# A layer of hybrid RG-LRU and neighbourhood attention on one core: 36 weight loads go from SyncE's queue to ScalarE's

## The chip, the core and the metric

The kernel runs on one core of a Trainium2 chip. The metric is the time of one execution in device microseconds (us), the median over several runs. Engines are called by the names that the profile uses: PE (TensorE, matrix products; PEld are its weight loads), DVE (VectorE), ACT (ScalarE), POOL (GpSimd) and SP (SyncE, which here only issues DMA transfers). SPq is SP's queue of instructions.

## The reference

One layer over 512 tokens of 1024 features, in float32:

```python
x = x + 0.5 * swiglu_1(rmsnorm(x))
h = rmsnorm(x)
xr, gr, q, k, v, ga, gb = split(h @ w_in, 7)      # 1024 columns each
xc = conv4(xr)                                    # centred, depthwise
y_lru = (scan_forward(xc) + scan_backward(xc)) * gelu(gr)
q = rmsnorm_per_head(q) * 64**-0.5; k = rmsnorm_per_head(k)
y_att = neighbourhood_attention(q, k, v, rel_pos_bias)  # 16 heads, window 8 rows x 16 columns
x = x + (sigmoid(ga) * y_lru + sigmoid(gb) * y_att) @ w_out
x = x + 0.5 * swiglu_2(rmsnorm(x))
```

## The kernel before

Features lie on the 128 partitions and tokens along the row. Every float32 operand of a product is split into a rounded high part and a low rest, and each product is three matrix products (high by high, high by low, low by high). The weights come in chunks of 128 x 1024 (512 KB). `load_w` (lines 159 to 169) loads one: a DMA fills a raw buffer, ACT casts it to the high part `wh` (line 145) and DVE subtracts to get the low part `wl` (line 148). There are three raw buffers and four pairs of `wh` and `wl`. So the load of chunk i waits until the `wl` of chunk i-3 is made, and the cast of chunk i waits until TensorE is done with chunk i-4; if nothing holds the loads back, up to seven chunks are on their way or ready ahead of TensorE.

The layer runs in stages: the first feed-forward block, the projection xr with its convolution, then q, k and v in two halves of eight heads (`hf` 0 and 1, lines 1101 to 1111; 12 chunks in each half), then the three gates (`gates`, line 1114: 24 chunks `wg`, 8 each for gr, ga and gb), w_out, and the second feed-forward block. The scans and the attention are laid between the chunks: `weave` (line 577) takes so many steps of each of five lists after each chunk and in its middle, at rates set by hand for each stage.

The attention of one half (`heads`, line 937) makes four tiles of two heads each (`fi` 0 to 3). For a tile, ACT and DVE split q and k into `qh`, `ql`, `kh`, `kl` (lines 961 to 966), TensorE makes the scores (line 989), DVE and ACT the softmax (lines 1009 to 1021), DVE transposes the result (lines 1030, 1031), SP writes it to memory (`pd<-pt`, line 1033), POOL reads it back turned (`PT<-pd`, line 1037), TensorE applies it to v (line 1052), and ACT copies the result out (`att`, line 1062). In the second half q and k are not turned on TensorE: DVE transposes blocks (line 916), SP writes them to memory (`qd`, line 919), and SP fetches each tile two tiles ahead (`xqk<-qd`, line 933, four DMAs for each tile).

The order of instructions on each engine's queue is settled when the program is built: a planner walks the program and at each moment gives an engine the ready instruction that stands first in the program, except those put under a high priority, by its own reckoning of times. The casts and subtractions of `load_w` have high priority; its DMA has not. On the chip every queue keeps that order, and an instruction that has to wait holds all that stand behind it in its queue. In the kernel before, SP's queue holds nearly all loads of weights (line 163), the writes of v (line 863), `qd` (919), the fetches of q and k (933) and the writes of the softmax (1033).

Of the kernel before, what the change touches and what calls it, by code (L numbers as in the profile page):

```python
# [91 lines left out]
def block_kernel(ctx: ExitStack, tc, a, out):  # L92
    nc = tc.nc
# [14 lines left out]
    def nm(s):  # L108
        uid[0] += 1
        return f"{s}_{uid[0]}"  # L110
# [32 lines left out]
    def split(raw, H, L, act=True):  # L143
        if act:
            nc.scalar.activation(H, raw, AF.Copy)  # L145
        else:
            nc.vector.tensor_copy(H, raw)
        return nc.vector.tensor_tensor(L, raw, H.bitcast(F32), ALU.subtract)  # L148

    nld = [0]  # L150

    def raw_t():
        return wpool.tile([P, 1024], F32, tag="wraw", bufs=3, name=nm("wraw"))

    def hl_t():
        return (wpool.tile([P, 1024], F32R, tag="wh", bufs=4, name=nm("wh")),
                wpool.tile([P, 1024], F32R, tag="wl", bufs=4, name=nm("wl")))

    def load_w(src, n, act=True):
        raw = raw_t()  # L160
        H, L = hl_t()
        s = slice(0, n)
        ld = nc.sync.dma_start(raw[:, s], src[:, s])
        if nld[0] < 8:
            tc.keep_in_program_order(ld)
        nld[0] += 1
        with tc.high_priority():
            split(raw[:, s], H[:, s], L[:, s], act)
        return H, L
# [6 lines left out]
    def feat_chunk(src, nk, xh, xl, ps, k0, ktot, act=True, mid=None):  # L176
        H, L = load_w(src, nk * P, act)
        for k in range(nk):
            s = slice(k * P, (k + 1) * P)
            kk = k0 + k  # L180
            mm3(ps, H[:, s], L[:, s], xh[kk], xl[kk], kk == 0, kk == ktot - 1)
            if mid is not None and k == nk // 2 - 1:
                weave(mid)
# [241 lines left out]
    def ffn(wgu, ws, wd, xh, xl, S, ssum, plain, res, emit_out, lead=None, end=None):  # L425
# [86 lines left out]
        for q in range(2):  # L512
# [19 lines left out]
            for j in range(FT // 2):  # L532
                ws_.append(load_w(wd[q, j], 1024))
                ahead(q * FT + 2 * j + 2 + AHEAD)
                if j < FT // 2 - DTAIL:
                    for k in (2 * j, 2 * j + 1):
                        for i in range(4):
                            put_in(i, k)
# [58 lines left out]
    def load_pairs():  # L597
        for k in range(KT):
            if k % 2 == 0:
                q = pair_t()  # L600
            xres[k] = q[:, k % 2]
# [107 lines left out]
    def lru():  # L709
# [14 lines left out]
        def fetch(f):  # L724
            wts[f] = load_w(a["wgate"][f], 2 * P)
# [115 lines left out]
    def qk_raw(w, hf, st):  # L841
        raws = []
        for ps in tok_group(w, hf):
            t = big_t(n="qk")
            with tc.high_priority():
                copy = nc.scalar.activation(t, ps, AF.Copy)  # L846
            raws.append(t)
        for j, t in enumerate(raws):
            sq = big.tile([P, T], F32, tag="pt", bufs=2, name=nm("sq"))
            after(nc.scalar.activation(sq, t, AF.Square), copy)  # L850
            nc.vector.reduce_sum(st[:, w, j, :], sq.rearrange("p (h d) -> p h d", d=HD), axis=AX.X)
        weave(RATE[phase[0]])
        return raws

    def v_get(hf):
        for j, ps in enumerate(tok_group(2, hf)):
            t = big_t(n="v")
            with tc.high_priority():
                nc.vector.tensor_scalar(t, ps, rcol[:, j : j + 1], None, ALU.mult)
            V[hf, 2 * j] = t  # L860

        for j in range(NCB):
            nc.sync.dma_start(vd[hf][:, j * QC : (j + 1) * QC, :], V[hf, 2 * j])
        lanes["v"].append(v_more(hf))
        if hf == 0:
            until("v", lambda: False)
        weave(RATE[phase[0]])
# [31 lines left out]
    def norm_qk(raws, st, qd):  # L899

        rq = tiny.tile([P, 2, NCB, 8], F32, tag="rq", name=nm("rq"))
        for w in range(2):
            for j in range(NCB):
                hold(nc.vector.tensor_scalar(rq[:, w, j, :], st[:, w, j, :], 1.0 / HD, epsv[:, j : j + 1],
                                             ALU.mult, ALU.add))
        hold(nc.scalar.activation(rq, rq, AF.Sqrt))
        nc.vector.reciprocal(rq, rq)
        yield
        for j in range(NCB):
            for w in range(2):  # L910
                t = raws[w][j].rearrange("p (h d) -> p h d", d=HD)
                hold(nc.vector.tensor_tensor(t, t, rq[:, w, j, :].unsqueeze(2).to_broadcast([P, 8, HD]), ALU.mult))
            if qd is not None:
                t2 = pair_t().rearrange("p a b -> p (a b)")
                for w in range(2):
                    nc.vector.transpose(
                        t2.rearrange("p (c f w i) -> p w f c i", c=NCB, f=4, w=2)[:, w],
                        raws[w][j].rearrange("p (f c i) -> p f c i", c=NCB, i=32))
                nc.sync.dma_start(qd[j], t2)
                yield  # L920
            elif j % 2 == 1:
                yield
        if qd is not None:
            yield
            fetch(qd, 0)
            fetch(qd, 1)
# [174 lines left out]
    for hf in range(2):  # L1101
        st = tiny.tile([P, 2, NCB, 8], F32, tag="st", name=nm("st"))
        raws = [qk_raw(0, hf, st), qk_raw(1, hf, st)]
        if hf == 1:
            qd = dram.tile([NCB, P, NCB, 4, 64], F32, name="qd")
            lanes["prep"].append(norm_qk(raws, st, qd))
        v_get(hf)
        if hf == 0:
            lanes["att"].append(norm_qk(raws, st, None))
        lanes["att"].append(heads(hf, raws, qd if hf == 1 else None))  # L1110
        phase[0] = "t1" if hf == 0 else "g"


    def gates(w, fs, fn, scale=1.0):
# [34 lines left out]
            yl.append(L)  # L1149


    nxt = {}
    load_pairs()
    forms = Forms(C_G2)
# [103 lines left out]
```

## Time and profile before

| | us |
|---|---|
| median of 3 runs | 1118.76 |
| lowest and highest run | 1116.25, 1119.7 |
| the profiled execution, its own time | 1117.62 |
| its span, first to last instruction | 1115.8 |
| PE busy | 1096.9 (98%) |
| ACT busy | 619.1 (55%) |

The profile is of one execution. In the views below, a start is in us from the start of the span. A timeline merges instructions of one kind that follow each other, with their count. Issuing a DMA is not counted as busy time of an engine. What stands in brackets is the time for which the engine was idle before the instruction, and what ended it. The granted clock is the share of TensorE's full clock: 1.00 is 2.4 GHz, 0.50 is 1.2 GHz.

### The profile page before, as it was taken

How to read it: one execution, taken by the hardware profiler on the slowest of the kernel's cores; microseconds unless marked ns; L12 is line 12 of the kernel's file. 1: busy time of each engine (PE TensorE's matmuls, PEld its weight loads, DVE VectorE, ACT ScalarE, POOL GpSimd, SP SyncE). 2: the span in 40 equal slices, each digit the busy share in tenths (PEclk: the TensorE clock that was granted, in tenths of full speed). 3: DMA queues.
4: the chain of work that ended last, by engine and by line, in shares of the span. 5: the costliest groups of instructions: out<-in, count | busy, mean ns of one | idle time of the engine just before them, and what ended most of it. 6: DMA issues, size and time to landing. Idle time of an engine off the chain costs nothing.

```text
span 1115.8 us, 17664 instructions
## 1 busy us (share of the span) xinstructions
PE 1096.9 (98%) x6779; PEld 971.5 (87%) x6779; DVE 796.1 (71%) x1228; ACT 619.1 (55%) x950; POOL 140.0 (13%) x243
## 2 busy tenths in 40 slices
PE   9999999999999999999999699999999999999998
PEld 8899999988888778787878488888999999998887
DVE  7777777794745877998786474759877777784642
ACT  8554554563533768877688482446645444564330
POOL 0000000000000441241226320001000000000000
PEclk9999999999999999999999799999999999999999
DMA  8566666643423685674789853376756666653421
GB/s 268 151 169 152 154 152 167 167 136 95 135 87 112 173 234 157 179 197 128 231 266 231 251 183 128 105 246 156 197 147 162 155 167 147 157 169 95 132 76 38
DMA packets 68451, 180.02 MB, mean 161 GB/s; under 512 B 17680, under 2 KB 21264, under 8 KB 68368
## 3 DMA queue, kind: packets, MB, share of 16 engines
q1 hardware_dynamic: 52160, 131.94, 36.4%
q0 software_dynamic: 15632, 46.70, 20.9%
q8 instruction: 53, 0.87, 0.3%
q10 hardware_dynamic: 576, 0.26, 0.1%
q14 instruction: 30, 0.25, 0.1%
HBM read 152.63 MB, written 17.83 MB: 153 GB/s over the span
## 4 chain that ended last, share of the span: by engine, by line
PE 93%; DVE 3%; ACT 2%; DMA 2%; issue 1%; SPq 0%; DVEq 0%; ACTq 0%
PE acc L312 31%; PE acc L172 10%; PE acc L174 9%; PE acc L173 9%; PE aux L312 5%; PE acc L834 4%; PE aux L173 4%; PE aux L172 4%; PE aux L174 4%; PE acc L835 4%; PE acc L836 4%; PE aux L742 1%; PE aux L1052 1%; DMA vd<-v 1%; ACT p L1021 1%
## 5 line engine op out<-in xcount | busy, mean ns | idle before, releaser
L145 ACT ACTIVATE wh<-wraw 128x1024 fp32r<-128x1024 f32 (+3 forms) x236 | 233.3, 991 | 322.2 <-issue 88.7
L148 DVE TENSOR_TENSOR wl<-wraw,wh 128x1024 fp32r<-128x1024 f32 (+3 forms) x236 | 267.5, 1137 | 111.4 <-ACT wh L145 107.7
L312 PE MATMUL acc<-s,wh 128*128 128x256 f32 x1280 | 232.2, 283 | 0.0
L312 PEld LDWEIGHTS acc<-s,wh 128*128 128x128 f32 x1280 | 199.7, 192 | 0.0
L312 PE MATMUL acc<-s,wl 128*128 128x256 f32 x640 | 181.1, 283 | 0.0
L312 PEld LDWEIGHTS acc<-s,wl 128*128 128x128 f32 x640 | 122.9, 192 | 0.0
L172 PE MATMUL acc<-xh,wh 128*128 128x512 f32 x272 | 108.6, 399 | 10.8 <-ACT wh L145 10.8
L174 PE MATMUL acc<-xh,wl 128*128 128x512 f32 x272 | 107.2, 394 | 0.0
L173 PE MATMUL acc<-xl,wh 128*128 128x512 f32 x272 | 107.0, 393 | 0.0
L312 PE MATMUL acc<-xh,wl 128*128 128x256 f32 x320 | 90.6, 283 | 0.0
L312 PE MATMUL acc<-xl,wh 128*128 128x256 f32 x320 | 90.6, 283 | 0.0
L312 PE MATMUL acc<-xh,wh 128*128 128x256 f32 x320 | 90.6, 283 | 0.0
L834 PE MATMUL acc<-wh,xh 128*128 128x512 f32 x192 | 75.7, 394 | 1.0 <-ACT qk L846 1.0
L148 DVE TENSOR_TENSOR hl<-h,hh 128x512 fp32r<-128x512 f32 x88 | 57.3, 686 | 25.4 <-PE aux L173 23.4
L835 PE MATMUL acc<-wh,xl 128*128 128x512 f32 x192 | 74.8, 390 | 0.0
L836 PE MATMUL acc<-wl,xh 128*128 128x512 f32 x192 | 74.7, 389 | 0.0
L172 PEld LDWEIGHTS acc<-xh,wh 128*128 128x128 f32 x272 | 51.7, 190 | 23.7 <-ACT wh L145 11.0
L172 PE MATMUL aux<-hh,wh 128*128 128x512 f32 (+1 forms) x181 | 69.9, 386 | 0.0
L173 PE MATMUL aux<-hl,wh 128*128 128x512 f32 (+1 forms) x181 | 69.9, 386 | 0.0
L174 PE MATMUL aux<-hh,wl 128*128 128x512 f32 (+1 forms) x181 | 69.9, 386 | 0.0
L174 PE MATMUL acc<-hh,wl 128*128 128x512 f32 (+1 forms) x176 | 67.9, 386 | 0.0
L173 PE MATMUL acc<-hl,wh 128*128 128x512 f32 (+1 forms) x176 | 67.9, 386 | 0.0
(226 smaller groups left out, 2301.8 us busy)
## 6 DMA issues: line engine op xcount, KB each, us to landing
wraw<-wqkv SPq DMA_DIRECT2D x24, 512.0 KB
wraw<-wg SPq DMA_DIRECT2D x24, 512.0 KB
wraw<-w1d SPq DMA_DIRECT2D x22, 512.0 KB
wraw<-w2s SPq DMA_DIRECT2D x22, 512.0 KB
pair<-w2s SPq DMA_DIRECT2D x22, 512.0 KB
wraw<-w2d SPq DMA_DIRECT2D x22, 512.0 KB
wraw<-w1s SPq DMA_DIRECT2D x18, 512.0 KB
pair<-w1s SPq DMA_DIRECT2D x18, 512.0 KB
```

The lines of the kernel that those rows point to most:

```text
L145: nc.scalar.activation(H, raw, AF.Copy)
L148: return nc.vector.tensor_tensor(L, raw, H.bitcast(F32), ALU.subtract)
L172: nc.tensor.matmul(ps, wh, xh, start=first, stop=False, skip_group_check=skip)
L173: nc.tensor.matmul(ps, wh, xl, start=False, stop=False, skip_group_check=skip)
L174: mark["mm"] = nc.tensor.matmul(ps, wl, xh, start=False, stop=last, skip_group_check=skip)
L312: mm = nc.tensor.matmul(o, w_[:, c], x_, start=first and m + k == 0 and w_ is H and x_ is xh_, stop=m + k == 4 and w_ is L, skip_group_che ...
L742: prev, mm = mm, nc.tensor.matmul(ps[d][b], W[w][o, c], X[x][o], start=x == 1, stop=w + x == 0)
L834: nc.tensor.matmul(pss[j], xh[kk][:, tj], H[:, s], start=kk == 0, stop=False)
L835: nc.tensor.matmul(pss[j], xl[kk][:, tj], H[:, s], start=False, stop=False)
L836: mark["mm"] = nc.tensor.matmul(pss[j], xh[kk][:, tj], L[:, s], start=False, stop=kk == KT - 1)
L1021: nc.scalar.activation(pt, pt, AF.Copy, scale=rs[:, hp, n : n + 1])
L1052: mm = nc.tensor.matmul(pv[h2 * HD : (h2 + 1) * HD, n * P : (n + 1) * P], vt[:, (fi * 2 + h2) * HD : (fi * 2 + h2 + 1) * HD], PT[:, q], st ...
```

## The change

The queue from which `load_w` issues its DMA becomes a variable: SP's as before, but from the end of the first half's pass (after its q, k, v and the start of its attention) ACT's, and SP's again ahead of w_out. So the 12 loads of the second half's q, k and v and the 24 loads of the gates are issued by ACT. The small loads of the scans' weights (`wgate`, line 725) go through `load_w` too; their last issue in the trace before lies at 431.7 us, ahead of the second half's first load. Buffers, dependences and the rest of the program are the same.

```diff
@@ -148,6 +148,7 @@
     nld = [0]
+    wq = [nc.sync]
@@ -160,7 +161,7 @@
         raw = raw_t()
         H, L = hl_t()
         s = slice(0, n)
-        ld = nc.sync.dma_start(raw[:, s], src[:, s])
+        ld = wq[0].dma_start(raw[:, s], src[:, s])
@@ -1109,6 +1110,7 @@
         lanes["att"].append(heads(hf, raws, qd if hf == 1 else None))
         phase[0] = "t1" if hf == 0 else "g"
+        wq[0] = nc.scalar
@@ -1149,6 +1151,7 @@
+    wq[0] = nc.sync
     nxt = {}
     load_pairs()
     forms = Forms(C_G2)
```

## Rows read from the trace of the kernel before

**Rows 1.** The page, parts 1 and 2: engine, busy us, share; then tenths in 40 slices.

```profile
PE 1096.9 (98%) x6779; PEld 971.5 (87%) x6779; DVE 796.1 (71%) x1228; ACT 619.1 (55%) x950; POOL 140.0 (13%) x243
...
PEclk9999999999999999999999799999999999999999
```

**Rows 2.** Waits of TensorE, 440 to 735 us: who waited for whom, us, times, longest.

```profile
PE acc L172 <- ACT wh L145: 10.8, 1, 10.8
PE aux L1052 <- issue: 1.9, 1, 1.9
PE acc L834 <- ACT qk L846: 1.0, 1, 1.0
PE aux L989 <- DVE kl L966: 0.3, 1, 0.3
```

**Rows 3.** Timeline of TensorE, 590 to 660 us: start us, us, instruction, [idle before it].

```profile
594.47 0.40 PE L989 MATMUL aux<-kl,qh 64*128 64x256 f32 x2 [0.32 <-DVE kl L966]
...
629.25 0.80 PE L172 MATMUL acc<-xh,wh 128*128 128x512 f32 x1 [10.78 <-ACT wh L145]
...
634.88 0.39 PE L172 MATMUL acc<-xh,wh 128*128 128x512 f32 x1
...
640.10 0.39 PE L174 MATMUL acc<-xh,wl 128*128 128x512 f32 x1
```

**Rows 4.** Stretches: busy us (instructions) of PE, PEld, DVE, ACT, POOL; granted clock; DMA share; GB/s.

```profile
575.00:585.00 10.00, 10.00 (x53) 8.01 (x52) 7.97 (x23) 9.57 (x19) 0.61 (x1) 1.00 1.00 319
585.00:595.00 10.00, 9.68 (x49) 7.77 (x49) 7.80 (x17) 8.57 (x18) 6.41 (x11) 1.00 0.80 225
595.00:605.00 10.00, 10.00 (x84) 8.50 (x82) 5.90 (x26) 9.92 (x27) 6.50 (x11) 1.00 1.05 237
...
622.00:630.00 8.00, 0.75 (x2) 0.50 (x2) 3.29 (x6) 1.06 (x1) 3.36 (x7) 0.50 1.01 346
```

**Rows 5.** Timeline of SyncE, 440 to 700 us: start us, us over all, DMA issues merged.

```profile
573.49 0.33 SPq L163 DMA_DIRECT2D wraw<-wg  x1
578.52 0.32 SPq L933 DMA_DIRECT2D xqk<-qd  x1
...
579.42 7.68 SPq L933 DMA_DIRECT2D xqk<-qd  x7
...
594.44 2.39 SPq L933 DMA_DIRECT2D xqk<-qd  x4
...
607.02 2.31 SPq L933 DMA_DIRECT2D xqk<-qd  x4
619.75 2.75 SPq L1033 DMA_DIRECT2D pd<-pt  x2
622.55 20.34 SPq L163 DMA_DIRECT2D wraw<-wg  x8
```

**Rows 6.** Timeline of VectorE, 565 to 650 us.

```profile
579.05 1.23 DVE L148 TENSOR_TENSOR wl<-wraw,wh 128x1024 fp32r<-128x1024 f32 x1 [1.06 <-ACT wh L145]
...
583.08 1.21 DVE L148 TENSOR_TENSOR wl<-wraw,wh 128x1024 fp32r<-128x1024 f32 x1
...
590.21 1.22 DVE L148 TENSOR_TENSOR wl<-wraw,wh 128x1024 fp32r<-128x1024 f32 x1
...
593.76 0.65 DVE L966 TENSOR_TENSOR kl<-xqk,kh 128x512 fp32r<-128x512 f32 x1
```

**Rows 7.** Timeline of ScalarE, 560 to 660 us.

```profile
620.99 0.57 ACT L1062 ACTIVATE att<-aux 128x512 f32<-128x512 f32 x1
628.14 1.06 ACT L145 ACTIVATE wh<-wraw 128x1024 fp32r<-128x1024 f32 x1 [6.59 <-DMA wraw<-wg]
```

**Rows 8.** Waits of SyncE's queue, 440 to 700 us.

```profile
SPq L163 <- DVE wl L148: 113.4, 29, 7.2
```

**Rows 9.** Lines 163 (452 to 513 us) and 446: engine, op, count, duration ns min/median/max, starts.

```profile
L163 SPq DMA_DIRECT2D wraw<-wqkv x12: 327/328/335, 453.4 to 507.0; - x12
...
L446 ACTq DMA_DIRECT2D wraw<-w1gu x3: 397/453/454, 1.2 to 2.1; - x3
```

## The prediction

> **What bounds the kernel now.** I read the page first. TensorE is busy for 1096.9 of the span's 1115.8 us [rows 1], so all that another order of queues can give back is 18.9 us of idle time, and what a lowered clock adds. The row of the granted clock shows where to look: it is at full in all slices of the middle but one, the 23rd, which begins 22 x 27.9 = 614 us into the span [rows 1].
>
> So the second view is TensorE's waits from 440 to 735 us, the stretch in which the moved loads are used. One wait stands out: 10.8 us for a cast of weights. The other three are 1.9, 1.0 and 0.3 us [rows 2]. The timeline of TensorE gives the place: it waits 10.78 us before the matmul at 629.25 [rows 3].
>
> The third view follows that cast back. ACT makes it at 628.14, after an idle time of 6.59 us that ended with the DMA of a chunk `wg` [rows 7]. SP issued that DMA at 622.55, and the one before at 573.49: 49 us without a load of weights [rows 5]. One chunk keeps TensorE busy for 24 matmuls of 0.227 us, that is 5.4 us (the 0.227 is worked out below). The seven chunks that the buffers hold ahead give 38 us and the scores between them a little more, so a gap of 49 us drains them.
>
> What held SP? Not the buffers. The `wl` at 579.05, 583.08 and 590.21 end at 580.3, 584.3 and 591.4 [rows 6]; each frees a raw buffer, so three loads could have gone out from 580 on. SP's own order held it: between the two loads of `wg` stand the fetches of q and k and the writes of the softmax, down to the pair that begins at 619.75 [rows 5]. Those wait for DVE's transposes, these for scores, and the scores for TensorE's place in its own order. The load stood behind a chain that the load itself doesn't need.
>
> **What the change takes away.** 36 loads leave SP's queue: 12 of the second half's q, k and v, issued from 453.4 to 507.0 [rows 9], and 24 of the gates. SP is left with the writes of v, `qd`, the fetches and the softmax. The chunk that came 49 us after its forerunner no longer stands behind these. I take it that the stall goes as a whole, in two terms:
>
> - The wait itself, 10.78 us [rows 3].
> - The slow clock behind it. From 622 to 630 us the granted clock is 0.50, which is 1.2 GHz, after TensorE had stood idle [rows 4]. From 629.25 to 634.88 run 12 matmuls in 5.63 us; from 634.88 to 640.10 run 23 in 5.22 us, 0.227 us each [rows 3]. Twelve at that rate are 2.72 us, so the clock costs 5.63 - 2.72 = 2.91 us.
>
> Together 13.7 us. What is late next, when the stall is gone: the other three waits, 3.2 us in sum [rows 2], of which the change may take some, since SP now writes v, `qd` and the softmax without a load in front. I count nothing for it and keep it for the low end.
>
> **What the change adds on ACT.** ACT gets 36 issues. On SP one takes 0.327 us [rows 9]; the three that ACT issues in the first us of the kernel take 0.397 to 0.454 us [rows 9], so 36 cost 11.8 to 16.3 us of ACT's queue. That is spread over 240 us. Where ACT is fullest it is busy for 9.57, 8.57 and 9.92 of 10 us [rows 4]. Between 575 and 595 two loads would go out, 2 x 0.45 = 0.9 us, and ACT's idle time there is 0.43 + 1.43 = 1.86 us: covered, taken as nothing. Were that cover gone, the 0.9 us would pass to `kl`, for which TensorE already waits 0.32 us at 594.47 [rows 3].
>
> Each issue also brings a wait onto ACT: for the `wl` of three chunks before. SP stood 113.4 us in 29 such waits, 3.9 us each, the longest 7.2 [rows 8]. On SP they were long because SP comes early. On ACT each load stands where the planner thought its buffer free, with the softmax, the casts and the copies out of PSUM queued behind it. The cost of one is between 0 and 7.2 us of ACT; on TensorE most of it is hidden, because casts run chunks ahead. It isn't hidden where TensorE waits for ACT in the same moment: the eight `qk` copies of the second half (line 846, already 1.0 us of waiting [rows 2]), the four splits of q and k, and the copies `att`. The trace of before can't show it; I take 0 in the likeliest case and price the rest as a rival.
>
> **What the change moves on the DMA engines.** The loads that were missing from 574 to 622 us are now in flight there, and the DMA engines are not idle: shares of 1.00, 0.80 and 1.05 in three of these stretches [rows 4], all of it without weights after the load at 573.49. When nearly nothing but weights ran, they moved 346 GB/s [rows 4], so 512 KB (0.524 MB) take 1.52 us of all engines. Two loads (buffers free at 580.3 and 584.3) come ahead of the scores at 594.47, which are fed by the fetches at 578.52 and 579.42 [rows 5] through `kl` at 593.76 [rows 6], with no slack (a wait of 0.32 us). If these fetches land later by the two loads, the scores are late by 2 x 1.52 = 3.0 us. The bounds are 0 (the fetches are issued first, and DVE and ACT, not the landing, may set `kl`) and 7.2 us (the longest wait of rows 8 in the same place). I take 3.0, the one that the rows price. Later crowding costs less: the next fetches, at 594.44 and 607.02, are two tiles ahead of use [rows 5].
>
> **The sum.** The profiled execution took 1117.62 us: 1115.8 of span and 1.8 around it. 1117.62 - 10.78 - 2.91 + 3.0 = 1106.9. It lies 1.1 us below the median of the runs shown, 1118.76, so on the median's scale the forecast is 1108.0.
>
> **A page that speaks against it.** The Trainium skill, page "DMA: Bandwidth & Descriptors", section "Issuing engines are not separate DMA queues", says that transfers issued from several engines run on the same 16 DMA engines anyway, and that a second issuing engine saves only the sequencer's time for the issue. By that rule SP would save 36 x 0.327 = 11.8 us that are not on the path, and the time would stay at 1118.8. The trace agrees that the transfers share their engines, but it shows a second thing which the rule leaves out, a queue that stands still for 49 us behind other waits [rows 5]. This is the first rival below.
>
> **Rivals.**
>
> 1. *The stall stays.* The load moves to ACT but keeps its place. For it: on ACT, too, the late cast at 628.14 stands behind the last work of the tile's softmax and the `att` copy at 620.99 [rows 7], and ACT takes earlier work of the program first; a load placed behind that softmax would be as late as before. Against it: the buffers were free by 580 to 591 [rows 6], and only SP's own queue stood between. Time: 1118.8, plus one or no wait of 3.9 us: 1115.4 to 1122.7. Chance 0.17.
>
> 2. *Only part of it goes.* The load is issued earlier, yet still late, or the scores' wait for `kl` takes over more than the 7.2 us of the bound. 1118.8 - 13.7 + 7.2 = 1112.3, up to 1115.4. Chance 0.05.
>
> 3. *ACT becomes the bound.* A load whose buffer isn't free stands at the head of ACT while TensorE needs a copy or a split behind it. There are 20 such places: 8 `qk` copies, 4 splits of q and k, 8 `att` copies; the 8 `qk` come in two groups of four that a single wait holds, so 14. With the stall gone, each costs 3.9 us at most in the mean: it is slower by over 0.3% once (13.7 + 3.4) / 3.9 = 4.4, so 5 of 14, are hit. With six to eight hit: 1118.8 - 13.7 + 23.4 to 31.2 = 1128 to 1136. With the stall still there, one place is enough, and two give 1126.6. For it: ACT is busy for over 95% in two of the four stretches of rows 4. Against it: TensorE waits for ACT's copies only 1.0 us in the whole stretch [rows 2], and the planner puts a load behind work that is ready. Chance 0.16.
>
> **How the numbers follow.** The forecast, a stall gone and some crowding, has 0.62. Its own range: 1118.8 - 13.7 - 3.2 = 1101.9 at the low end (no crowding, the other waits gone too) to 1118.8 - 13.7 + 7.2 = 1112.3. The 8-in-10 range takes in rivals 1 and 2 as well: 1102 to 1122.7, in which lie some 0.60 + 0.05 + 0.16. The chances are counted at 0.3% of 1118.8, 3.4 us, about what a measurement of this kernel can tell from no change. Faster (below 1115.4): 0.62 + 0.05 = 0.67, less 0.01 for overlap, 0.66. Within 0.3%: 0.16, nearly all of rival 1. Slower: 0.18, rival 3 with the far end of rival 1.
>
> **What would show it.** In the profile after: the loads on line 163 stand on ACT's queue, with no gap of some 45 us between two of `wg`; no wait of TensorE for a cast over 2 us; the granted clock 1.00 in every slice of that stretch; TensorE's idle time down from 18.9 to 8 to 11 us. Crowding shows as a wait of the second half's first scores for `kl`, of about 3 us. Rival 1 shows a `wg` load on ACT behind the softmax and the same long wait. Rival 3 shows ACT idle ahead of its loads, released by `wl`, and TensorE waiting for `qk`, `att` or `kl`. The prediction is wrong if the stall stays, or if the waits on ACT reach TensorE in five places or more.

## The result and the profile after

Twelve runs of each kernel, one beside the other on the same chip, give 1120.3 us after the change (1116.67 to 1122.49) and 1116.83 us before it. The ratio is 1.0027, with an interval of 1.0015 to 1.0039. The forecast was 1108.0 us. The change makes the kernel some 3 us slower. The interval doesn't reach down to 1, so there is a loss, but it is about the 0.3% that the prediction counted as no change, and far from the 10.8 us that were to be gained.

The page of the kernel after, parts 1, 2 and 3 (busy us of the engines, the granted clock in 40 slices, and the queues with their packets, MB and share of the DMA engines):

```profile
PE 1099.6 (98%) x6779; PEld 973.8 (87%) x6779; DVE 795.3 (71%) x1228; ACT 616.3 (55%) x948; POOL 139.9 (13%) x243
...
PEclk9999999999999999999988999999999999999999
...
q1 hardware_dynamic: 46976, 113.07, 30.8%
...
q10 hardware_dynamic: 5760, 19.13, 5.5%
```

The 36 loads are on ScalarE's queue: q10 now carries 19.13 MB. The span is 1119.1 us, so TensorE is idle for 19.5 us, as much as before (18.9, from [rows 1]). The low digit of the clock has moved from the 23rd slice to the 21st and 22nd. Something was taken away and something else put in its place. TensorE's waits from 440 to 745 us, after (to be read against [rows 2]):

```profile
PE aux L990 <- DVE kl L967: 6.1, 1, 6.1
PE aux L1053 <- DMA PT<-pd: 4.8, 1, 4.8
PE acc L835 <- ACT qk L847: 2.5, 2, 2.3
PE aux L990 <- DVE nmx L1010: 0.9, 1, 0.9
PE aux L953 <- DVE nmx L1010: 0.2, 1, 0.2
```

The wait for a cast, 10.8 us, has gone. In its place stand a wait for `kl`, the low half of the keys of the second half's first tile (0.3 before), one for `PT`, the turned softmax (1.9 before), and a longer one for `qk`. Where the time went is read by putting the same blocks of TensorE's work from both timelines beside each other:

| block of TensorE | start before | start after | later by |
|---|---|---|---|
| projection behind the `qk` copies | 524.80 | 526.46 | 1.7 |
| gate chunk behind the transposes for the last tile of the first half | 553.62 | 557.02 | 3.4 |
| gate chunk behind the `PT` wait | 573.62 | 580.72 | 7.1 |
| second half, scores of tile 0 | 594.47 | 609.47 | 15.0 |
| gate chunk behind these scores | 598.04 | 614.89 | 16.9 |
| product with v ahead of the old stall | 616.50 | 633.34 | 16.8 |
| chunk that had the old stall | 629.25 | 635.24 | 6.0 |
| second half, scores of tile 1 | 640.42 | 643.62 | 3.2 |

The stall and its slow clock gave back 16.84 - 3.20 = 13.64 us. Between 510 and 615 us 16.9 us were lost first. The difference, 3.3 us, is that of the two spans (1119.1 and 1115.8). The places on TensorE's timeline after, to which the answers to [rows 3] belong:

```profile
578.81 1.12 PE L1053 MATMUL aux<-PT,vs 128*64 128x128 f32 x8 [4.78 <-DMA PT<-pd]
...
609.47 0.58 PE L990 MATMUL aux<-kl,qh 64*128 64x256 f32 x2 [6.08 <-DVE kl L967]
...
614.89 0.50 PE L173 MATMUL acc<-xh,wh 128*128 128x512 f32 x1
...
635.24 0.50 PE L173 MATMUL acc<-xh,wh 128*128 128x512 f32 x1
```

The block at 609.47 takes 5.42 us up to 614.89; before, the same block took 598.04 - 594.47 = 3.57. The stretches say why (busy us and instructions of PE, PEld, DVE, ACT, POOL; granted clock; DMA share; GB/s):

```profile
575.00:585.00 10.00, 6.19 (x30) 5.08 (x31) 1.68 (x6) 1.99 (x5) 0.63 (x1) 0.66 0.79 250
...
605.00:615.00 10.00, 5.53 (x57) 5.14 (x58) 5.23 (x20) 8.22 (x19) 2.96 (x6) 0.66 0.87 241
```

In both the mean granted clock is 0.66: after each of the two longer waits TensorE ran on at 1.2 GHz for a while (a granted clock of 0.50 from 578.8 to 582.5 and from 609.5 to 613.5 us). These are the two low slices of the page.

What made `kl` late is read on ScalarE. Its timeline after, from 584 us to the split of the keys (`kh`), from which VectorE makes `kl`:

```profile
584.60 1.06 ACT L145 ACTIVATE wh<-wraw 128x1024 fp32r<-128x1024 f32 x1 [7.63 <-PE acc L174]
...
590.04 1.06 ACT L145 ACTIVATE wh<-wraw 128x1024 fp32r<-128x1024 f32 x1 [4.38 <-PE acc L174]
591.01 1.05 ACT L1126 ACTIVATE pair<-pair 128x1024 f32<-128x1024 f32 x1
...
603.20 1.06 ACT L145 ACTIVATE wh<-wraw 128x1024 fp32r<-128x1024 f32 x1 [0.27 <-PE acc L174]
604.17 0.70 ACT L962 ACTIVATE qh<-xqk,gq 128x512 fp32r<-128x512 f32 x1
604.89 1.28 ACT L1126 ACT_TABLE_LOAD   x1
606.18 1.06 ACT L1126 ACTIVATE pair<-pair 128x1024 f32<-128x1024 f32 x1
...
607.89 0.61 ACT L965 ACTIVATE kh<-xqk 128x512 fp32r<-128x512 f32 x1
```

ScalarE waits 7.63 and 4.38 us ahead of two casts, and what ends these waits is TensorE: the cast needs a buffer that TensorE has still to read. Behind the casts stand the softmax of the first half's last tile and then the split. Before `kh` a cast, a table load and a gate function (`pair`, line 1126) are also in the way. Over the whole stretch (who waited for whom, us, times, longest):

```profile
ACT wh L145 <- PE acc L174: 45.2, 15, 7.6
...
ACT L907 <- DVE wl L148: 1.8, 1, 1.8
ACT att L1063 <- DVE wl L148: 1.7, 1, 1.7
```

The first was 30.5 us in 10 times before, over the same 440 to 745 us. Not all of the difference is new waiting, since other matmuls of TensorE end such waits too: all waits of these casts for TensorE came to 46.5 us before and 57.0 after. The other two lines are all that the moved loads made ScalarE wait for a raw buffer: 3.5 us.

None of these instructions is in the diff. The lists of instructions of the two programs, put beside each other engine by engine, show how they come into it: of ScalarE's other 863 instructions 43 have another place, of VectorE's 104, of TensorE's 6639 only six. The planner settles the order by its own reckoning of times. A load that it reckons to land earlier makes its cast ready earlier, and casts (and VectorE's subtractions) have a high priority, so they move ahead of softmax and splits in the fixed lists. On the chip they then wait there for TensorE.

### The profile page after: what moved, and what is told of

It is laid out like the page before. It is cut to its first block, busy times and chain, and to the rows that moved or that the text cites. A ratio compares the mean times of both kernels' runs of the same rounds, so it can differ in the third digit from the quotient of the medians.

```text
span 1119.1 us, 17653 instructions
## 1 busy us (share of the span) xinstructions
PE 1099.6 (98%) x6779; PEld 973.8 (87%) x6779; DVE 795.3 (71%) x1228; ACT 616.3 (55%) x948; POOL 139.9 (13%) x243
## 3 DMA queue, kind: packets, MB, share of 16 engines
q10 hardware_dynamic: 5760, 19.13, 5.5%
## 4 chain that ended last, share of the span: by engine, by line
PE 95%; DVE 2%; DMA 1%; ACT 1%; issue 0%; POOL 0%; ACTq 0%
PE acc L313 31%; PE acc L173 11%; PE acc L174 10%; PE acc L175 10%; PE aux L313 5%; PE aux L175 4%; PE aux L173 4%; PE aux L174 4%; PE acc L835 3%; PE acc L836 3%; PE acc L837 3%; PE aux L1053 1%; PE aux L743 1%; PE aux L990 1%; DMA PT<-pd 1%; PE acc L465 1%
## 5 line engine op out<-in xcount | busy, mean ns | idle before, releaser
L173 PE MATMUL acc<-hh,wh 128*128 128x512 f32 (+1 forms) x176 | 68.0, 386 | 0.0
```

Of the source, the lines that this page charges most:

```text
L173: nc.tensor.matmul(ps, wh, xh, start=first, stop=False, skip_group_check=skip)
```

## The experiments

Three theories were set against each other for the 16.9 us. **A**: the changed order of ScalarE's other work costs them. **B**: the loads, now earlier, crowd the transfers that the scores and the softmax need. **C**: ScalarE's issues, and its waits for raw buffers, cost by themselves. Each time below is the median, with its ratio to the kernel before, run beside it on the same chip, and the interval.

**Half of the change each.** First the 12 loads of q, k and v alone, then the 24 loads of the gates alone:

```diff
# e1_qkv_only: back to SyncE ahead of the gates
+    wq[0] = nc.sync
# e2_gates_only: to ScalarE ahead of the gates, not after the first half
-        wq[0] = nc.scalar
+    wq[0] = nc.scalar
```

> The 12 loads of the second half's q, k and v on ACT, the 24 of the gates back on SP. Theory A (ACT's order: loads on ACT bring casts and gate functions ahead of the second half's split of q and k): the stall at the tenth gate chunk stays (about 10.8 us of wait and 2.9 us of slow clock), the wait of the first second-half scores for kl stays at about 0.3 us, the waits for qk and nmx may cost 1 to 3 us: 1117 to 1120 us. Theory B (crowding of the DMA engines by loads moved into a full stretch): nothing is moved there, 1117 us. Theory C (the issue on ACT and its wait for wl cost by themselves, in proportion to the loads): the stall stays and a third of after's loss of 17 us comes on top, 1122 us.

> The 24 loads of the gates on ACT, the 12 of the second half's q, k and v back on SP. Theory A: the stall is gone (13.7 us), the wait for kl stays at 5 to 7 us with its slow clock, what was lost before 550 us (some 3 us: waits for qk and nmx) goes: 1115 to 1118 us. Theory B: stall gone, the waits for PT (4.8) and kl (6.1) as in the changed kernel: 1118 to 1120 us. Theory C: stall gone and two thirds of the loss of 17 us: 1114 us.

With q, k and v alone: 1121.24 us, 1.0033 (1.0023 to 1.0044). The stall stays, as the waits of TensorE show, and the time rises all the same:

```profile
PE acc L173 <- ACT wh L145: 10.7, 1, 10.7
PE aux L1053 <- DMA PT<-pd: 3.4, 1, 3.4
```

With the gates alone: 1119.33 us, 1.0013 (0.9997 to 1.0029). The stall is gone, and the waits for `kl` (6.1 us), `PT` (4.0) and `qk` (2.8) are near those of the whole change. So the gates' loads carry the whole gain and most of the loss; the other twelve bring no gain, and 3.7 us of loss when they move alone.

**Hold two things back.** The cast and the gate function that had moved ahead of `kh` in the second half's first tile are held behind it; all other places stay.

```diff
@@ split: the cast waits for kh @@
+            if pin:
+                after(i, mark["kh0"])
...
@@ gate function @@
+            if "kh0" in mark and nld[0] > mark["n"] + 3:
+                after(i, mark["kh0"])
```

> The changed kernel, but on ACT one cast and one gate function (and all later ones) are held behind the split of k of the second half's first tile. Theory A: what stood between the two halves of that split (a table load of 1.28 us, a function of 1.06 us) and the cast ahead of it (1.06 us) no longer delay kl: the wait of 6.1 us falls to 2 to 4 us, 1115 to 1118 us. Theory B: the fetch lands late, the wait for kl stays near 6 us, 1119 to 1121 us. Theory C: as B.

1118.75 us, 1.0004 (0.9992 to 1.0017). The wait for `kl` falls from 6.08 to 3.90 us. Only five places differ in ScalarE's list and three in VectorE's, so 2.2 us of the wait are those two instructions; the rest comes from work ahead of them. The time itself differs from that of the change by no more than the intervals allow.

**The loads early, but on SyncE's queue.** They are put ahead of SyncE's other work by a high priority instead of being moved to another engine.

```diff
-        ld = wq[0].dma_start(raw[:, s], src[:, s])
+        with nullcontext() if wq[0] is nc.sync else tc.high_priority():
+            ld = nc.sync.dma_start(raw[:, s], src[:, s])
...
-        wq[0] = nc.scalar
+        wq[0] = None
```

> The loads stay on SP, but are put under high priority, so that they go between the fetches of q and k instead of behind them; ACT's order up to the split of the second half's first tile is that of the kernel before. Theory A: the stall goes (13.7 us) and nothing is lost on ACT: 1103 to 1107 us, the wait for kl under 2 us. Theory B: the same loads crowd the same stretch, PT and kl come late as in the changed kernel: 1113 to 1119 us, waits of 3 to 6 us for each. Theory C: no ACT issue, so 1103 to 1107 us.

1108.51 us, 0.9922 (0.9904 to 0.994): faster than both kernels, and close to the time that the prediction gave to the change. The waits of TensorE in the whole stretch:

```profile
PE aux L1054 <- DMA PT<-pd: 2.9, 2, 2.3
PE acc L836 <- ACT qk L848: 1.0, 1, 1.0
PE aux L991 <- DVE kl L968: 0.3, 1, 0.3
PE aux L991 <- ACT att L1064: 0.2, 1, 0.2
```

The stall is gone, and `kl` is waited for no longer than before. Two loads of `wg` go out at 581.06 and 586.51 (575.60 and 586.95 in the change), just ahead of the scores, and with them B doesn't give 6 us at `kl`.

**ScalarE's list exchanged.** In e6 the loads stay on ScalarE and its other work is held in the order of the kernel before; in e7 the loads stand as in e5, on SyncE, and ScalarE's work is held in the order of the change. The list is written out, and each instruction made to follow the one before it in the list:

```diff
+    for one, two in zip(ORDER, ORDER[1:]):
+        after(seen[f"I-{two}"], seen[f"I-{one}"])
```

> The changed kernel, its 36 loads on ACT, with one thing added: the casts, functions and softmax steps of ACT are held by order edges in the order in which they stand on ACT in the kernel before; only the loads are slipped in between. Theory A (the moved order on ACT costs the 17 us): the stall is gone and the loss too, 1103 to 1110 us, wait for kl under 2 us. Theory B (the DMA engines are crowded by loads moved into a full stretch): 1114 to 1120 us, waits for PT and kl of 4 to 6 us as in the changed kernel. Theory C (the issue on ACT and its wait for wl): 1114 to 1120 us.

> The converse: loads on SP under high priority as in e5_sp_first (1108.5 us), with ACT's other work held in the order in which it stands in the changed kernel. Theory A: the waits of the changed kernel come back, for kl 4 to 7 us, 1115 to 1121 us. Theory B and theory C: as e5_sp_first, 1106 to 1110 us, since neither the DMA engines nor ACT's issues are touched.

e7: 1115.64 us, 0.9988 (0.9979 to 0.9997), 7 us over e5 without one of the moved loads issued on ScalarE. The wait for `kl` is back, and ScalarE's timeline shows the same row of work ahead of `kh` as in the change:

```profile
PE aux L1003 <- DVE kl L980: 6.2, 1, 6.2
```

```profile
595.99 1.05 ACT L110 ACTIVATE wh<-wraw 128x1024 fp32r<-128x1024 f32 x1
596.94 0.71 ACT L110 ACTIVATE qh<-xqk,gq 128x512 fp32r<-128x512 f32 x1
597.67 1.28 ACT L110 ACT_TABLE_LOAD   x1
598.96 1.06 ACT L110 ACTIVATE pair<-pair 128x1024 f32<-128x1024 f32 x1
...
600.67 0.61 ACT L110 ACTIVATE kh<-xqk 128x512 fp32r<-128x512 f32 x1
```

e6: 1120.77 us, 1.0035 (1.0022 to 1.0048). Here A as I had put it was wrong: for the time as a whole the old order is no cure. Up to the scores of tile 0 it is one in the main: the wait for `kl` falls to 3.2 us, and the gate chunk behind these scores starts at 603.15, 5.1 us later than before, where the change is 16.9 late. What is lost again lies behind it. Part of the stall is back, 4.8 us for a cast and 1.9 for a `wl`, though the loads are on ScalarE. The timeline of ScalarE shows the late cast, not waiting for its load, but standing behind the softmax and the `att` copy of the tile, where the old list has it:

```profile
626.82 0.57 ACT L110 ACTIVATE att<-aux 128x512 f32<-128x512 f32 x1
627.30 2.94 ACT L110 ACTIVATE wh<-wraw 128x1024 fp32r<-128x1024 f32 x3
```

So moving the load takes the stall away only because the planner also moves the cast forward; the gain and the loss come out of the same re-ordering.

**The issues alone.** The kernel before, with 36 additional transfers of 4 bytes for each partition, issued by ScalarE beside the moved loads, each behind the cast before it.

```diff
+        if issue[0] is not None:
+            m = nc.scalar.dma_start(mute[:, issue[0] : issue[0] + 1], src[:, 0:1])
+            after(m, mark["cast"])
+            issue[0] += 1
```

> The kernel before, all loads on SP, with 36 more issues on ACT: beside each of the 36 loads ACT issues a DMA of 4 bytes for each partition into a column that nobody reads, behind the cast of the load before. It prices ACT's issue alone, without its wait for wl. Theory A and theory B: within 2 us of the kernel before, 1116 to 1119.5 us. Theory C: 36 x 0.334 = 12 us on ACT, of which 4 us or more reach TensorE: 1121 us or more.

1120.74 us, 1.0029 (1.0016 to 1.0041), but not by the issues: up to the scores of tile 0 the timeline is only 0.9 us later than before, at 0.334 us an issue. The rest is the old stall, which grew from 10.8 to 15.9 us in the profiled execution (1122.93 us). SyncE's late load was issued at 623.88, and the cast that waits for it began at 634.13:

```profile
634.13 1.06 ACT L145 ACTIVATE wh<-wraw 128x1024 fp32r<-128x1024 f32 x1 [11.24 <-DMA wraw<-wg]
```

**Fewer transfers.** The change, without 14 of the 16 loads of the attention's bias, which fall into the same stretch.

```diff
+            if g:
+                bms[g, hp] = bms[0, hp]
+                continue
```

> The changed kernel without 14 of the 16 loads of the relative bias (320 KB each, 4.6 MB between 500 and 640 us): all heads use the bias of the first two, so that part of the output is another. ACT's order is that of the changed kernel. Theory A: the wait for kl stays at 4 to 6.5 us, 1116 to 1120 us. Theory B: with 4.6 MB less the waits for PT and kl fall by half or more: 1110 to 1114 us. Theory C: 1118 to 1120 us.

1119.4 us, 1.0016 (1.0004 to 1.0029). The wait for `kl` stays at 6.1 us; that for `PT` falls from 4.8 to 3.1. Crowding by these loads is worth 1.7 us at the turned softmax and nothing at `kl`; the gate chunk behind the scores of tile 0 starts 3.1 us earlier than in the change (611.77).

**e5's order with the loads on ScalarE.** In e9 ScalarE's other work alone is held in e5's order; e5 ran again beside it. In e10 the lists of all five engines are held, in e11 those of ScalarE and VectorE. The edit is that of e6 with other lists. VectorE's list comes out near e5's only where it is held, and not wholly there: 112 of its instructions stand elsewhere than in e5 in e9, 37 in e10 and 36 in e11. TensorE's list is the planner's in e9 and e11.

> The changed kernel, its 36 loads on ACT, with ACT's other work held in the order in which it stands in e5_sp_first (1108.5 us): the casts are early there, but those of the chunks that TensorE needs late stand behind the split of q and k. e6_old_order held the order of the kernel before, which has the late cast in it, and so kept part of the stall; this one doesn't. Theory A (the order on ACT costs, not the queue): 1106 to 1112 us, wait for kl under 2.5 us, no wait for a cast over 2 us. Theory C (ACT's issues and their waits for wl cost by themselves): 1114 to 1121 us. Theory B (crowding): 1108 to 1114 us, with waits for PT of 4 us or more.

> e5_sp_first once more, beside e9_good_order on the same chip: 1106 to 1110 us by every theory. The difference of the two is what the queue costs when ACT's order is the same.

> The loads are on ScalarE's queue, as in the changed kernel, and all other work of ScalarE, TensorE, VectorE, GpSimd and SyncE is held in the order in which e5 has it (there the loads stay on SyncE's queue, ahead of other work; 1108.5 and 1110.0 us). Only the 36 issues stand on another engine. Theory A, all that the change loses comes from the changed order of the engines' other work: 1106 to 1112 us, TensorE waits for the first keys of the second half (kl) under 2.5 us, as in e5, and for no weight half over 2 us. Theory C, a load that stands on ScalarE costs by itself, by its issue and by its wait until VectorE has read the buffer: 1114 to 1121 us, with idle time of ScalarE ahead of its loads that VectorE's wl ends, of more than 3 us a time, and TensorE's waits for kl behind them of 3 us or more. Theory B, crowding of transfers: as A, since the loads come no earlier than in e5.

> As e10 (loads on ScalarE's queue), but only ScalarE's and VectorE's other work is held in e5's order; TensorE's, GpSimd's and SyncE's lists are left as the planner makes them. It tells which engine's order makes up the 8 us between e9 (ScalarE's list alone held, 1120.3) and e10 (every list held, 1112.4). If it is VectorE's list, with the splits of the keys standing behind the low halves of the weights in it: 1109 to 1114 us, and TensorE's waits for kl under 2.5 us each. If it is the place of TensorE's own scores and transposes in its list: 1117 to 1121 us, with waits for kl of 3 us or more as in e9. One wait of 3 to 5 us for qk near 528, behind a load that waits at ScalarE's head, is expected either way.

| | median us | ratio | interval |
|---|---|---|---|
| e9, ScalarE's list held | 1120.3 | 1.0024 | 1.001 to 1.0038 |
| e11, ScalarE's and VectorE's | 1113.46 | 0.9964 | 0.9952 to 0.9975 |
| e10, all lists | 1112.37 | 0.9945 | 0.9926 to 0.9963 |
| e5 again, loads on SyncE | 1110.01 | 0.9938 | 0.9924 to 0.9953 |

TensorE's waits in e9, then in e10:

```profile
PE aux L1002 <- DVE kl L979: 8.3, 3, 3.8
PE aux L1065 <- issue: 2.8, 1, 2.8
PE acc L847 <- ACT qk L110: 2.2, 2, 1.8
```

```profile
PE acc L118 <- ACT qk L118: 4.2, 1, 4.2
PE aux L118 <- DMA PT<-pd: 1.9, 1, 1.9
PE aux L118 <- DVE kl L118: 0.3, 1, 0.3
```

For the time as a whole e9 speaks against A if A means ScalarE's list alone: `kl` is still late, three times. With VectorE's list held as well (e11) 7 us are back, and the waits for `kl` are 2.1 us in sum; holding the other lists too adds no more than the intervals allow. So A stands in a wider form: it is the order of ScalarE and VectorE together.

For the 16.9 us themselves ScalarE's list does more than the times show. The gate chunk behind the scores of tile 0 starts at 598.04 before; in the other runs:

| | starts at, us | later than before | span, us |
|---|---|---|---|
| the change | 614.89 | 16.9 | 1119.1 |
| e6, ScalarE's list as before | 603.15 | 5.1 | 1117.5 |
| e9, ScalarE's list as in e5 | 604.82 | 6.8 | 1116.9 |
| e11, VectorE's too | 604.66 | 6.6 | 1113.1 |
| e10, all lists | 603.91 | 5.9 | 1110.6 |
| e7, loads on SyncE, ScalarE's list of the change | 607.91 | 9.9 | 1113.6 |
| e5, loads on SyncE, first and second execution | 600.28, 600.59 | 2.2, 2.6 | 1107.6, 1108.2 |

With the loads on ScalarE and its list held, 10.1 us (e9) and 11.8 us (e6) of the 16.9 are gone; with the list of the change and the loads on SyncE, e7 is 7.6 us later than e5. The planner lays VectorE's list anew around a list that is held (153 of its instructions stand elsewhere than in the change in e9, 142 in e6), so this isn't ScalarE's list by itself. What e11 gains over e9 comes behind this place, where the two are 0.2 us apart.

In this second execution of e5 crowding does show at `kl`, where the first had 0.3 us: ScalarE's split of q waits for the fetch, and TensorE then 2.41 us for `kl`:

```profile
593.79 0.72 ACT L963 ACTIVATE qh<-xqk,gq 128x512 fp32r<-128x512 f32 x1 [3.03 <-DMA xqk<-qd]
```

What is left between e10 and e5 is small: the intervals overlap, and the two spans differ by 2.4 us (1110.6 and 1108.2). e10's one large wait, 4.2 us for `qk` where e5 has 1.0, is C, at one place. ScalarE's timeline there:

```profile
515.68 5.19 ACTq L118 DMA_DIRECT2D wraw<-wg  x2
520.89 1.28 ACT L118 ACT_TABLE_LOAD   x1 [4.71 <-DVE wl L118]
522.19 0.46 ACT L118 ACTIVATE p<-so,nmx 128x192 f32<-128x192 f32 x1
```

A load stands at the head of ScalarE's list until VectorE's `wl`, which ends at 520.5, has freed the raw buffer. The table load, the softmax, the splits and the `qk` copies stand behind it. With the slow clock after that wait (0.50 from 528.2 to 532.0 us) it makes up most of the 5.9 us by which e10 is late.

## Why the prediction was wrong

**The stall: right, in place and size.** It was to give 10.78 + 2.91 = 13.7 us; the blocks moved back by 13.64. No wait of TensorE for a cast is left.

**The cost on ScalarE: the step that failed.** The prediction put it as "the planner puts a load behind work that is ready" and took 0 for what the moved loads do to ScalarE. It priced the 36 issues and the 36 waits, and both were small: the issues 0.9 us up to tile 0 in e8, the waits 3.5 us of ScalarE. It did not ask what the planner does with the instructions that follow a load. Casts and subtractions with a high priority, ready earlier in the planner's reckoning, were moved ahead of the softmax and of the splits of q and k. The sum lacks this term. It is most of the 16.9 us, slow clock included: holding ScalarE's list takes 10.1 to 11.8 of them away with the loads left on ScalarE (e9, e6), and all lists 11.0 (e10). In the other direction ScalarE's list of the change, with the other lists laid anew around it, costs e5 7 us (e7). In the time as a whole 8 us come back, in steps, from e9 over e11 to e10. Not all of it is shown to be order: e5, with the loads early but on SyncE, is 2.2 to 2.6 us late at the same place, for which nothing here singles out a cause, and e10 some 3.5 us more, mostly by one load at the head of ScalarE's list. How the part of the order divides between ScalarE's list and VectorE's isn't settled either: no run held VectorE's list alone.

**The crowding of 3.0 us at `kl`: real, but not what made `kl` late here.** With the old places of the splits (e5) TensorE waits for `kl` 0.3 us in one execution, as before, and 2.4 in another, so the term was of the right kind and its 3.0 us above both. In the change the splits come so late that the fetches have long landed: ahead of `qh` at 604.17 and `kh` at 607.89 ScalarE waits for no DMA. The prediction named a wait for `kl` of about 3 us as the sign of crowding; the 6.1 us that appeared would have been misread by it, and e4, which takes transfers away, leaves them as they are. At `PT`, which the sum left out, crowding cost 1.7 us (e4).

**The rivals.** Rival 3, ScalarE as the bound, had the right engine and the wrong mechanism: its sign, ScalarE idle ahead of its loads and released by `wl`, came to 3.5 us in the change. The wait that did grow was that of its casts for TensorE, from 46.5 to 57.0 us. Its own mechanism was seen in e10, at one of the 14 places, for 4.7 us on ScalarE and 3.2 on TensorE; the prediction's 3.9 us for a place was about right for the wait, but left out the slow clock behind it. Rival 1, the stall stays, gives nearly the measured time, but by something that did not happen. Its reason was sound: e6 shows that the late cast, kept in its place, brings back part of the stall wherever the load is issued.

The Trainium skill, page "DMA: Bandwidth & Descriptors", section "Issuing engines are not separate DMA queues", would have had the time stay at 1118.8 us, since another issuing engine saves only the time of the issue. The measured time is near that, yet the trace doesn't bear the rule out as the reason: the queue that stood still did cost 13.6 us, and e5 gets some 8 us of it back without a second issuing engine. Two effects of opposite sign, 13.6 and 16.9 us, happen to cancel.

**The other signs.** The loads are on ScalarE's queue, as forecast. The granted clock was to be full throughout and is 0.66 in two stretches; TensorE's idle time was to fall to 8 to 11 us and is 19.5. The 1108 us that the sum gave are near the time of e5, in which the loads come early and the splits keep their place. The gain of 10.8 us isn't reached there either: e5's spans are 8.2 and 7.6 us shorter than that of the kernel before, against the stall's 13.6. Of the difference 2.2 to 2.6 us are lost up to tile 0; the rest, behind it, wasn't followed.

## What to carry to other kernels

When a planner lays out the queues, a load that moves takes with it every instruction that becomes ready with it: before you price the move, list the work that depends on the load, ask which of it has priority, and what it will be put in front of. A load that is late because of its place in a queue can be given a better place in that same queue; another engine's queue is worth its order, not just its idle time. Before you trust such a gain, put the two instruction lists side by side, engine by engine: here a diff of four lines moved over a hundred instructions that it doesn't name.

## What the hardware showed besides

- Two of TensorE's waits cost more than their length. After those of 4.78 and 6.08 us the granted clock was 0.66 in the mean of the 10 us around, and the block of scores behind the second took 5.42 us instead of 3.57.
- The same load of 512 KB, late in the same place, was followed by its cast 5.59 us after its issue before ([rows 5, 7]: 622.55, 628.14) and 10.25 us after it in e8. Between issue and cast the DMA engines were full in both, with shares of 1.01 and 1.00, and SyncE's queue moved as much, 1.85 and 1.81 MB. What differs is GpSimd's queue: it moved 0.12 MB in that time before and 1.41 MB in e8, where three loads of the bias went out at 621.09 (617.85 before) and reads of the turned softmax from 624.45 (626.64 before).
- An issue takes 0.334 us on ScalarE's queue in this stretch and 0.328 on SyncE's: the 0.40 to 0.45 us of [rows 9], from the start of the kernel, were too high.
